# A down product in seven half-size products in place of eight, in a one-core hybrid decoder layer

## The chip, the cores and the metric

One core of one Trainium2 chip. The metric is the device time of one execution in microseconds (us). Engines: PE (matrix products, with its weight loads shown as PEld), DVE (vector), ACT (scalar), POOL (GpSimd), SP (which here only issues DMAs). A matmul here multiplies a stationary 128x128 block by a moving block of up to 512 columns and adds into a PSUM bank of 512 float32 columns.

## The reference, cut to what matters

One layer: three token mixers side by side, merged and added to the stream `z`, then a convolution FFN. 512 tokens, 1024 channels, 2816 hidden units; everything is float32 in and out. The change concerns the last line of the FFN:

```python
def _conv_ffn(h, w_up, conv_w, conv_b, w_down):
    u = h @ w_up                       # 1024 -> 2 x 2816
    ...                                # causal convolution over 3 tokens, per unit
    gate, val = c[..., :D_FF], c[..., D_FF:]
    return (jax.nn.silu(gate) * val) @ w_down     # 2816 -> 1024
...
z = z + _conv_ffn(_rmsnorm(z, ffn_norm[i]), ...)
return _rmsnorm(z, final_norm)[:, N_META:]
```

## The kernel before

Every float32 product is done as three float16 products: both operands are split into a high part (rounded by ACT) and a low part (the remainder, by DVE), and high x high, high x low and low x high are summed in PSUM.

The FFN has two parts. In the up part, 22 turns `f` (L1717) each compute two gemms of 128 hidden units (gate and value) over all tokens into a two-bank PSUM tile (`gbank()`, a ring of two such tiles, g0 and g1), ACT copies each result out into a tile `u` (`evac`, L414), DVE runs the convolution (L1712, L1714) into a tile `c`, ACT applies silu (L1732), DVE multiplies (L1733), and ACT and DVE split the result into the float16 tile `hid` (L1734, L1735): unit tile `f` in rows, 512 tokens in columns. The tiles of w_up come through `weights` (L227, L233, L234): load into one of three buffers `wf` (512 KB each, a ring), then split into one of three tiles `w`.

The down part loads the 22 tiles of w_down (128 units x 1024 channels, 512 KB each) through the same three `wf` buffers (L1746), splits each into its own place in `wd` (L1747 on ACT, L1748 on DVE), all 22 of which stay in SBUF. The product runs first for the token tiles 0 and 1: unit by unit, 12 matmuls for each, into four single banks `dn` (L1789). Then come token tiles 2 and 3, one half of the channels at a time, into g0 and g1 (L1797). A matmul's stationary operand is a 128-token block of `hid`, its moving operand a 512-channel half of `wd`. `finish_half` adds the product to `z` (L1765), squares it (L1767) and multiplies it by the final norm's weights `fnb` (L1770); `finish` adds the two halves' sums and takes the root on POOL (L1773, L1774), scales the halves on DVE and ACT (L1776, L1777) and stores them (L1780).

The engines run their queues in order. The order within each queue is set when the program is built: `TileContext(nc, schedule_with_timeline_sim=True)` takes instructions by their place in the text, and lets later ones go first where its own timeline sees the earlier one wait. The matmul calls go through the helper class `Paced`, so all matmuls have the line L101.

Of the kernel before, what the change touches and what calls it, by code (L numbers as in the profile page):

```python
# [9 lines left out]
F16 = mybir.dt.float16  # L10
# [8 lines left out]
P = 128  # L19
# [106 lines left out]
def trunk(ctx: ExitStack, tc: tile.TileContext, d: dict, out: bass.AP):  # L126
# [1565 lines left out]
    hid = fp.tile([P, 2, KF, SEQ], F16, name="hid")  # L1692
# [14 lines left out]

    def conv(j, ps):
        u = ft.tile([P, NY], F32, tag="u", name=f"u{j}")
        evac(u, ps, LATE, scale=IWS)  # L1710
        c = ft.tile([P, SEQ], F32, tag="c", name=f"c{j}", bufs=3)
# [5 lines left out]
    for f in range(KF):  # L1717
# [16 lines left out]
        act.activation(hid[:, 0, f], cv, AF.Copy)  # L1734
        vec.tensor_tensor(hid[:, 1, f], cv, hid[:, 0, f], op=ALU.subtract)  # L1735
# [4 lines left out]
    KF1 = 18  # L1740
    wd1 = fp.tile([P, KF1, 2, D], F16, name="wd1")
    wd2 = dq.tile([P, KF - KF1, 2, D], F16, name="wd2")
    wd = [wd1[:, f] for f in range(KF1)] + [wd2[:, f] for f in range(KF - KF1)]
    for f in range(KF):
        wf = take_wf().rearrange("p a b -> p (a b)")
        sp.dma_start(wf, d["w_down"][0][P * f : P * (f + 1), :])  # L1746
        act.activation(wd[f][:, 0], wf, AF.Copy, scale=WS)  # L1747
        vec.scalar_tensor_tensor(wd[f][:, 1], wf, WS, wd[f][:, 0], ALU.mult, ALU.subtract)  # L1748

    fnb = fp.tile([P, D], F32, name="fnb")  # L1750
    sp.dma_start(fnb, d["final_norm"].rearrange("(o c) -> o c", o=1).broadcast_to([P, D]))

    def down(pss, t, f, ss=(0, 1)):
        for j, (x, w) in enumerate(((0, 0), (0, 1), (1, 0))):
            for s in ss:
                pe.matmul(
                    pss[s], lhsT=hid[:, x, f, P * t : P * (t + 1)], rhs=wd[f][:, w, 512 * s : 512 * (s + 1)],
                    start=(f == 0 and j == 0), stop=(f == KF - 1 and j == 2),
                )

    def finish_half(pss, t, s, ss):
# [3 lines left out]
        vec.scalar_tensor_tensor(z, pss[s], IWS / HS, z, ALU.mult, ALU.add)  # L1765
        sq = ft.tile([P, NY], F32, tag="u", name=f"sq_{t}{s}")
        act.activation(sq[:, 0:512], z, AF.Square, scale=1.0 / 32, accum_out=ss[:, s : s + 1])  # L1767
        if s == 0:
            gps.tensor_scalar(ss[:, 0:1], ss[:, 0:1], EPS, None, ALU.add)  # L1769
# [12 lines left out]
    def sums(t):  # L1782
        return ft.tile([P, 2], F32, tag="ssf", name=f"ssf_{t}")


    pair = []
    for t in range(2):
        pair.append([bank(f"dn{t}{s}", P, 512) for s in range(2)])
    for f in range(KF):  # L1789
        for t in range(2):  # L1790
            down(pair[t], t, f)
    for t in range(2):
        ss = sums(t)
        for s in range(2):
            finish_half(pair[t], t, s, ss)
# [40 lines left out]
```

## Time and profile before

| | |
|---|---|
| median of 3 runs | 1013.29 us (1011.54 to 1013.64) |
| profiled execution | 1013.14 us, of which the span 1011.4 |
| PE, share of the span | 97% |
| DVE, ACT, POOL | 63%, 46%, 14% |
| granted PE clock, mean | 0.993 |
| HBM read | 86.92 MB |

Busy shares are averages over stages that have different limits, so what a change in one stage is worth is read in that stage: which engine works without a hole there, what the others wait for, and when the data that it needs are in place. Durations of pipelined instructions overlap: 264 matmuls of 379 ns each lie in 57 us.

### The profile page before, as it was taken

What the parts mean: (1) busy time and instruction counts of PE and PEld (TensorE: products, weight loads), DVE (VectorE), ACT (ScalarE), POOL (GpSimd) and SP (SyncE); (2) the same over time, 40 slices, a digit from 0 to 9 for tenths busy, and PEclk for the clock granted to TensorE, in tenths of its full rate; (3) what the DMA queues carried; (4) which work ended last, traced back from release to release, by engine and by line L of the source; (5) the groups of instructions that cost most, each with busy time, mean ns of one, the idle gap of its engine ahead of it and who ended that gap; (6) DMA issues with size and microseconds to landing.
All of it is one profiled execution on the core that took longest, in us unless ns stands there. A gap on an engine that the chain in (4) does not pass through costs nothing.

```text
span 1011.4 us, 20895 instructions
## 1 busy us (share of the span) xinstructions
PE 981.4 (97%) x8694; PEld 777.5 (77%) x8694; DVE 636.0 (63%) x1234; ACT 466.7 (46%) x881; POOL 136.8 (14%) x307
## 2 busy tenths in 40 slices
PE   8999999999999998999999999999999999999996
PEld 7888878888788777888888874488888888854442
DVE  5677655646678986767644494567776776872211
ACT  6867576347654344354433353643444344452100
POOL 3122221202335410111000032100000000000100
PEclk9999999999999999999999999999999999999999
DMA  6422222332244324122133562033233333573100
GB/s 194 108 64 63 66 66 82 84 84 80 79 111 108 92 73 91 39 64 64 43 84 94 183 206 66 1 105 104 87 103 105 104 92 98 161 218 101 42 21 21
DMA packets 149289, 92.35 MB, mean 91 GB/s; under 512 B 17664, under 2 KB 142073, under 8 KB 149195
## 3 DMA queue, kind: packets, MB, share of 16 engines
q1 hardware_dynamic: 149195, 91.02, 31.5%
q8 instruction: 68, 1.11, 0.5%
q14 instruction: 26, 0.21, 0.1%
HBM read 86.92 MB, written 3.95 MB: 90 GB/s over the span
## 4 chain that ended last, share of the span: by engine, by line
PE 78%; DVE 12%; ACT 5%; DMA 3%; issue 2%; POOL 1%; SPq 0%; POOLq 0%; DVEq 0%; ACTq 0%
PE g L101 60%; PE dn L101 6%; DVE w L234 2%; PE pc L101 1%; DVE HV L1222 1%; DVE AN L1227 1%; PE pf L101 1%; DVE wol L1606 1%; ACT w L233 1%; PE pw L101 1%; DMA s<-X 1%; ACT L414 1%; PE hT L106 1%; PE pogl L101 1%; PE pohg L101 1%
## 5 line engine op out<-in xcount | busy, mean ns | idle before, releaser
L101 PEld LDWEIGHTS <-w 128*128 128x128 f16 x5856 | 567.5, 98 | 86.1 <-issue 5.8
L101 PE MATMUL g<-hT,w 128*128 128x256 f16 (+3 forms) x5280 | 610.1, 274 | 1.3 <-DVE acc L478 0.6
L234 DVE SCALAR_TENSOR_TENSOR w<-wf,w 128x1024 f16<-128x1024 f32 (+1 forms) x131 | 150.5, 1150 | 91.5 <-ACT w L233 91.2
L233 ACT ACTIVATE w<-wf 128x1024 f16<-128x1024 f32 (+1 forms) x131 | 130.6, 999 | 109.7 <-PE g L101 100.2
L101 PEld LDWEIGHTS <-hid 128*128 128x128 f16 x528 | 51.7, 98 | 63.0 <-issue 1.1
L101 PE MATMUL g<-y,w 128*128 128x258 f16 x576 | 71.1, 273 | 1.4 <-DVE gate L478 1.3
L1714 DVE SCALAR_TENSOR_TENSOR c<-u,parB,c 128x512 f32<-128x512 f32 x88 | 66.0, 750 | 2.4
L101 PE MATMUL g<-wd,hid 128*128 128x512 f16 x264 | 57.3, 379 | 0.8 <-DVE z L1765 0.8
L101 PE MATMUL dn<-wd,hid 128*128 128x512 f16 x264 | 57.1, 379 | 0.0
L1769 POOL TENSOR_SCALAR ssf<-ssf 128x1 f32<-128x1 f32 x4 | 2.2, 540 | 311.2 <-ACT sq L1767 311.1
L101 PE MATMUL g<-woh,mT 128*128 128x512 f16 x128 | 38.9, 379 | 0.6 <-DVE z L1668 0.6
L1732 ACT ACTIVATE c<-c 128x512 f32<-128x512 f32 x22 | 13.8, 628 | 53.8 <-DVE c L1714 53.8
L1767 ACT ACTIVATE sq<-z 128x512 f32<-128x512 f32 x8 | 5.0, 628 | 71.5 <-DVE z L1765 71.5
L1748 DVE SCALAR_TENSOR_TENSOR wd<-wf,wd 128x1024 f16<-128x1024 f32 x22 | 26.9, 1223 | 16.5 <-ACT wd L1747 16.4
L101 PEld LDWEIGHTS <-mT 128*128 128x128 f16 x192 | 18.5, 98 | 24.2 <-issue 2.9
L1747 ACT ACTIVATE wd<-wf 128x1024 f16<-128x1024 f32 x22 | 23.2, 1057 | 25.9 <-DMA wf<-in_w_down_dram 25.9
L1765 DVE SCALAR_TENSOR_TENSOR z<-g,z 128x512 f32<-128x512 f32 x4 | 2.8, 692 | 45.8 <-PE g L101 45.8
L1468 POOL TENSOR_TENSOR gv<-gv,mhalf 128x2 f32<-128x2 f32 (+1 forms) x16 | 12.4, 779 | 128.3 <-DVE gv L1467 128.3
L414 ACT ACTIVATE u<-g 128x258 f32<-128x258 f32 x88 | 29.1, 372 | 0.0
L1497 ACT ACTIVATE HV<-pc 64x128 f32<-64x128 f32 x32 | 8.6, 270 | 36.6 <-DVE HV L1496 31.8
L101 PE MATMUL g<-wol,mT 128*128 128x512 f16 x64 | 24.3, 379 | 0.0
L1712 DVE TENSOR_SCALAR c<-u,parB 128x512 f32<-128x512 f32 x44 | 23.8, 541 | 0.0
(485 smaller groups left out, 1180.1 us busy)
## 6 DMA issues: line engine op xcount, KB each, us to landing
wf<-in_w_in_dram SPq DMA_DIRECT2D x65, 512.0 KB
wf<-in_w_up_dram SPq DMA_DIRECT2D x44, 512.0 KB
wf<-in_w_down_dram SPq DMA_DIRECT2D x22, 512.0 KB
wf<-in_w_out_dram SPq DMA_DIRECT2D x8, 512.0 KB
xt<-in_x_dram SPq DMA_DIRECT2D x4, 512.0 KB
wf<-in_w_out_hg_dram SPq DMA_DIRECT2D x8, 256.0 KB
wf<-in_w_out_gla_dram SPq DMA_DIRECT2D x8, 256.0 KB
wf<-in_w_out_rw_dram SPq DMA_DIRECT2D x8, 256.0 KB
```

Of the source, the lines that this page charges most:

```text
L101: r = self.eng.matmul(out, lhsT=lhsT, rhs=rhs, **kw)
L106: r = self.eng.transpose(out, in_, ident)
L233: act.activation(wh[:, :kt, :m], wf[:, :kt, :m], AF.Copy, scale=WS)
L234: vec.scalar_tensor_tensor(wl[:, :kt, :m], wf[:, :kt, :m], WS, wh[:, :kt, :m], ALU.mult, ALU.subtract)
L414: act.activation(dst[:m, off + c0 : off + c0 + n], src, func, **kw)
L1222: eng.tensor_tensor(u, bc(mats[:, j, j + 1 : n], c1 - c0), Ti[:, j, c0:c1].unsqueeze(1).broadcast_to([cnt, r, c1 - c0]), op=ALU.mult)
L1468: gps.tensor_tensor(var, var, mhalf[:, 0 : 2 * n].rearrange("p (a b) -> p a b", b=2), op=ALU.pow)
L1712: vec.tensor_scalar(c, u[:, 0:SEQ], colB(52 + j), colB(8 + j), ALU.mult, ALU.add)
L1714: vec.scalar_tensor_tensor(c, u[:, t : t + SEQ], colB(52 + 44 * t + j), c, ALU.mult, ALU.add)
L1732: act.activation(cg, cg, AF.Silu)
L1747: act.activation(wd[f][:, 0], wf, AF.Copy, scale=WS)
L1748: vec.scalar_tensor_tensor(wd[f][:, 1], wf, WS, wd[f][:, 0], ALU.mult, ALU.subtract)
```

## The change

The product Y = H W (H: tokens x units, W: units x channels) is computed block by block. H's blocks are halves of the tokens by the even and odd unit tiles of a pair; W's are the even and odd tile by halves of the channels. For each of 11 pairs:

- from H: A11, A12, A22 as they are, S1 = A21 + A22, S2 = S1 - A11, S3 = A11 - A21, S4 = A12 - S2 (`operands`, float32 sums on POOL, then all seven are split into high and low). `hid` holds seven blocks of 256 tokens for each pair;
- from W: T1 = B12 - B11, T2 = B22 - T1, T3 = B22 - B12, T4 = T2 - B21, and B11, B21, B22 as they are. `first_weights` makes T1 and T4 on POOL and T2 on DVE in place in `wf` and splits the two tiles; `last_weights` loads the odd tile again and half of the even tile, makes T3 on POOL and splits;
- seven products, each summed over the pairs in two banks (256 tokens x 512 channels): A11 B11, S2 T2, S1 T1, A22 T4 in a first stage; S3 T3 and S4 B22 in a second one, A12 B21 in a third. Between the stages ACT and DVE take the first four sums out of PSUM and add them to the four quarters of `z` as the scheme asks.

Split weights no longer stay for the whole product: 13 places (`NS1` + `NS2`) of a whole tile take turns. The tile `c` has four buffers in place of three. The load of `fnb` stands behind the first stage's.

```diff
@@ -1689,7 +1689,10 @@
     fctx = ExitStack()
     fp = fctx.enter_context(tc.tile_pool(name="ffn", bufs=1))
     ft = fctx.enter_context(tc.tile_pool(name="ffnt", bufs=2))
-    hid = fp.tile([P, 2, KF, SEQ], F16, name="hid")
+    HSEQ, KP = SEQ // 2, KF // 2
+    A11, A12, A22, S1, S2, S3, S4 = range(7)
+    hid = fp.tile([P, 2, KP, 7, HSEQ], F16, name="hid")
     w_up = d["w_up"][0]
     def up_gemm(j, ps, wt, spans):
@@ -1705,10 +1708,25 @@
     def up_weights(j):
         return weights(((w_up[:, P * j : P * (j + 1)], 0),), KD)
+    CB = 4
+    def operands(p, e, o):
+        e1, e2, o1, o2 = e[:, :HSEQ], e[:, HSEQ:], o[:, :HSEQ], o[:, HSEQ:]
+        sm = ft.tile([P, 4, HSEQ], F32, tag="sm", name=f"sm{p}", bufs=1)
+        gps.tensor_tensor(sm[:, 0], e2, o2, op=ALU.add)
+        gps.tensor_tensor(sm[:, 1], sm[:, 0], e1, op=ALU.subtract)
+        gps.tensor_tensor(sm[:, 2], e1, e2, op=ALU.subtract)
+        gps.tensor_tensor(sm[:, 3], o1, sm[:, 1], op=ALU.subtract)
+        for a, n, src in ((A11, 1, e1), (A12, 2, o), (S1, 4, sm.rearrange("p a t -> p (a t)"))):
+            h, l = (hid[:, x, p, a : a + n].rearrange("p a t -> p (a t)") for x in range(2))
+            act.activation(h, src, AF.Copy)
+            vec.tensor_tensor(l, src, h, op=ALU.subtract)
     def conv(j, ps):
         u = ft.tile([P, NY], F32, tag="u", name=f"u{j}")
         evac(u, ps, LATE, scale=IWS)
-        c = ft.tile([P, SEQ], F32, tag="c", name=f"c{j}", bufs=3)
+        c = ft.tile([P, SEQ], F32, tag="c", name=f"c{j}", bufs=CB)
         vec.tensor_scalar(c, u[:, 0:SEQ], colB(52 + j), colB(8 + j), ALU.mult, ALU.add)
         for t in (1, 2):
             vec.scalar_tensor_tensor(c, u[:, t : t + SEQ], colB(52 + 44 * t + j), c, ALU.mult, ALU.add)
@@ -1731,42 +1749,79 @@
         cg, cv = (conv(j, ps) for j, ps in zip(js, pss))
         act.activation(cg, cg, AF.Silu)
         vec.scalar_tensor_tensor(cv, cg, HS, cv, ALU.mult, ALU.mult)
-        act.activation(hid[:, 0, f], cv, AF.Copy)
-        vec.tensor_tensor(hid[:, 1, f], cv, hid[:, 0, f], op=ALU.subtract)
+        if f % 2:
+            operands(f // 2, cve, cv)
+        cve = cv
     h2ctx.close()
     dctx = ExitStack()
     dq = dctx.enter_context(tc.tile_pool(name="wd2", bufs=1, side="right"))
-    KF1 = 18
-    wd1 = fp.tile([P, KF1, 2, D], F16, name="wd1")
-    wd2 = dq.tile([P, KF - KF1, 2, D], F16, name="wd2")
-    wd = [wd1[:, f] for f in range(KF1)] + [wd2[:, f] for f in range(KF - KF1)]
-    for f in range(KF):
-        wf = take_wf().rearrange("p a b -> p (a b)")
-        sp.dma_start(wf, d["w_down"][0][P * f : P * (f + 1), :])
-        act.activation(wd[f][:, 0], wf, AF.Copy, scale=WS)
-        vec.scalar_tensor_tensor(wd[f][:, 1], wf, WS, wd[f][:, 0], ALU.mult, ALU.subtract)
+    NS1, NS2 = 10, 3
+    wd1 = fp.tile([P, NS1, 2, D], F16, name="wd1")
+    wd2 = dq.tile([P, NS2, 2, D], F16, name="wd2")
+    slots = [wd1[:, j] for j in range(NS1)] + [wd2[:, j] for j in range(NS2)]
+    NS = NS1 + NS2
+    nxt = 2 * KP % NS
+    take_slot = ring(NS, lambda j: slots[j])
+    take_t3 = ring(4, lambda j: slots[(nxt + j // 2) % NS][:, :, 512 * (j % 2) : 512 * (j % 2 + 1)])
+    take_last = ring(NS - 2, lambda j: slots[(nxt + 2 + j) % NS])
+    w_down = d["w_down"][0]
+    def rows(f, c0=0, n=D):
+        wf = take_wf().rearrange("p a b -> p (a b)")[:, :n]
+        sp.dma_start(wf, w_down[P * f : P * (f + 1), c0 : c0 + n])
+        return wf
+    def split_d(wf, w):
+        act.activation(w[:, 0], wf, AF.Copy, scale=WS)
+        vec.scalar_tensor_tensor(w[:, 1], wf, WS, w[:, 0], ALU.mult, ALU.subtract)
+        return w
+    lo, hi = slice(0, 512), slice(512, 1024)
+    def first_weights(p):
+        we, wo = rows(2 * p), rows(2 * p + 1)
+        gps.tensor_tensor(we[:, hi], we[:, hi], we[:, lo], op=ALU.subtract)
+        vec.tensor_tensor(wo[:, hi], wo[:, hi], we[:, hi], op=ALU.subtract)
+        gps.tensor_tensor(wo[:, lo], wo[:, hi], wo[:, lo], op=ALU.subtract)
+        we, wo = split_d(we, take_slot()), split_d(wo, take_slot())
+        return we[:, :, lo], we[:, :, hi], wo[:, :, hi], wo[:, :, lo]
+    def last_weights(p):
+        wo, wt = rows(2 * p + 1), rows(2 * p, 512, 512)
+        gps.tensor_tensor(wt, wo[:, hi], wt, op=ALU.subtract)
+        wo, wt = split_d(wo, take_last()), split_d(wt, take_t3())
+        return wo[:, :, lo], wo[:, :, hi], wt
     fnb = fp.tile([P, D], F32, name="fnb")
-    sp.dma_start(fnb, d["final_norm"].rearrange("(o c) -> o c", o=1).broadcast_to([P, D]))
-    def down(pss, t, f, ss=(0, 1)):
-        for j, (x, w) in enumerate(((0, 0), (0, 1), (1, 0))):
-            for s in ss:
+    def product(ps, a, w, p, ts=(0, 1)):
+        for t in ts:
+            for j, (x, y) in enumerate(((0, 0), (0, 1), (1, 0))):
                 pe.matmul(
-                    pss[s], lhsT=hid[:, x, f, P * t : P * (t + 1)], rhs=wd[f][:, w, 512 * s : 512 * (s + 1)],
-                    start=(f == 0 and j == 0), stop=(f == KF - 1 and j == 2),
+                    ps[t], lhsT=hid[:, x, p, a, P * t : P * (t + 1)], rhs=w[:, y],
+                    start=(p == 0 and j == 0), stop=(p == KP - 1 and j == 2),
                 )
-    def finish_half(pss, t, s, ss):
+    SC = IWS / HS
+    def add_to(t, s, v):
+        z = zt[t + 1][:, 512 * s : 512 * (s + 1)]
+        vec.scalar_tensor_tensor(z, v, SC, z, ALU.mult, ALU.add)
+    def finish_half(t, s, ss):
         hc = slice(512 * s, 512 * (s + 1))
         z = zt[t + 1][:, hc]
-        vec.scalar_tensor_tensor(z, pss[s], IWS / HS, z, ALU.mult, ALU.add)
         sq = ft.tile([P, NY], F32, tag="u", name=f"sq_{t}{s}")
         act.activation(sq[:, 0:512], z, AF.Square, scale=1.0 / 32, accum_out=ss[:, s : s + 1])
-        if s == 0:
-            gps.tensor_scalar(ss[:, 0:1], ss[:, 0:1], EPS, None, ALU.add)
+        if s == 1:
+            gps.tensor_scalar(ss[:, 1:2], ss[:, 1:2], EPS, None, ALU.add)
         vec.tensor_tensor(z, z, fnb[:, hc], op=ALU.mult)
     def finish(t, ss):
@@ -1780,29 +1835,58 @@
             sp.dma_start(out[0, P * t : P * (t + 1), hc], z[:, hc])
     def sums(t):
-        return ft.tile([P, 2], F32, tag="ssf", name=f"ssf_{t}")
-    pair = []
+        return ft.tile([P, 2], F32, tag="ssf", name=f"ssf_{t}", bufs=4)
+    def pair(name):
+        return [bank(f"{name}{t}", P, 512) for t in range(2)]
+    def gpair():
+        g = gbank()
+        return [g[:, 0, :], g[:, 1, :]]
+    q1, q6, q5, q4 = pair("q1"), pair("q6"), gpair(), gpair()
+    for p in range(KP):
+        b11, t1, t2, t4 = first_weights(p)
+        for ps, a, w in ((q1, A11, b11), (q6, S2, t2), (q5, S1, t1), (q4, A22, t4)):
+            product(ps, a, w, p)
+    sp.dma_start(fnb, d["final_norm"].rearrange("(o c) -> o c", o=1).broadcast_to([P, D]))
+    us = []
     for t in range(2):
-        pair.append([bank(f"dn{t}{s}", P, 512) for s in range(2)])
-    for f in range(KF):
-        for t in range(2):
-            down(pair[t], t, f)
+        u = ft.tile([P, SEQ], F32, tag="c", name=f"q16_{t}", bufs=CB)
+        v = ft.tile([P, SEQ], F32, tag="c", name=f"q165_{t}", bufs=CB)
+        act.activation(u, q1[t], AF.Copy)
+        vec.tensor_tensor(u, q6[t], u, op=ALU.add)
+        vec.tensor_tensor(v, q5[t], u, op=ALU.add)
+        us.append((u, v))
     for t in range(2):
-        ss = sums(t)
+        u, v = us[t]
+        z = zt[3 + t][:, lo]
+        vec.scalar_tensor_tensor(z, q4[t], -SC, z, ALU.mult, ALU.add)
+        for j, s, x in ((2 + t, 1, v), (2 + t, 0, u), (t, 1, v), (t, 0, q1[t])):
+            add_to(j, s, x)
+    b21s = []
+    for p in range(KP):
+        b21, b22, t3 = last_weights(p)
+        b21s.append(b21)
+        product(q6, S3, t3, p)
+        product(q5, S4, b22, p)
+    sss = [sums(t) for t in range(4)]
+    for t in range(2):
         for s in range(2):
-            finish_half(pair[t], t, s, ss)
-        finish(t, ss)
-    for t in range(2, 4):
-        g = gbank()
-        pss = [g[:, 0, :], g[:, 1, :]]
-        ss = sums(t)
-        for s in range(2):
-            for f in range(KF):
-                down(pss, t, f, (s,))
-            finish_half(pss, t, s, ss)
-        finish(t, ss)
+            add_to(2 + t, s, q6[t])
+            finish_half(2 + t, s, sss[2 + t])
+        finish(2 + t, sss[2 + t])
+    for t in range(2):
+        add_to(t, 1, q5[t])
+        finish_half(t, 1, sss[t])
+    for t in range(2):
+        for p in range(KP):
+            product(q1, A12, b21s[p], p, (t,))
+        add_to(t, 0, q1[t])
+        finish_half(t, 0, sss[t])
+        finish(t, sss[t])
     dctx.close()
     fctx.close()
```

## Rows read from the trace of the kernel before

**Rows 1.** The page's engine totals: busy us, share of the span, instructions.

```profile
PE 981.4 (97%) x8694; PEld 777.5 (77%) x8694; DVE 636.0 (63%) x1234; ACT 466.7 (46%) x881; POOL 136.8 (14%) x307
```

**Rows 2.** The chain that ended last, from 888 us: start, us, what.

```profile
888.71 56.98 PE dn L101 x264
945.70 42.75 PE g L101 x198
...
989.21 14.42 PE g L101 x66
...
1003.65 0.70 DVE z L1765
```

**Rows 3.** Busy us by stretch: PE, PEld, DVE, ACT, POOL; clock, DMA, GB/s.

```profile
864.00:889.00 25.00, 25.00 (x227) 21.81 (x225) 18.85 (x24) 13.07 (x22) 0.00 (x0) 1.00 0.55 169
889.00:905.00 16.00, 16.00 (x76) 7.26 (x75) 14.35 (x18) 9.20 (x13) 0.00 (x0) 1.00 0.75 233
905.00:925.00 20.00, 20.00 (x94) 9.06 (x93) 11.03 (x9) 8.69 (x9) 0.00 (x0) 1.00 0.60 181
925.00:944.00 19.00, 19.00 (x89) 8.62 (x88) 0.00 (x0) 0.00 (x0) 0.00 (x0) 1.00 0.00 1
```

**Rows 4.** The tile wd: instructions (ns min/median/max, starts); waits (us, times).

```profile
L1747 ACT ACTIVATE wd<-wf x22: 1056/1057/1057, 867.8 to 922.5; 128x1024 f16<-128x1024 f32 x22
L1748 DVE SCALAR_TENSOR_TENSOR wd<-wf,wd x22: 1214/1225/1226, 868.9 to 923.6; 128x1024 f16<-128x1024 f32 x22
...
  DMA wf<-in_w_down_dram: 25.9, 20
```

**Rows 5.** The timeline, 864 to 923: start us, us, engine, line; idle before, releaser.

```profile
864.31 55.22 SPq L1746 DMA_DIRECT2D wf<-in_w_down_dram  x22
...
867.80 1.06 ACT L1747 ACTIVATE wd<-wf 128x1024 f16<-128x1024 f32 x1 [0.35 <-DMA wf<-in_w_down_dram]
...
887.27 1.23 DVE L1748 SCALAR_TENSOR_TENSOR wd<-wf,wd 128x1024 f16<-128x1024 f32 x1 [2.48 <-ACT wd L1747]
...
888.41 0.64 ACT L414 ACTIVATE u<-g 128x258 f32<-128x258 f32 x2
...
893.52 0.64 ACT L414 ACTIVATE u<-g 128x258 f32<-128x258 f32 x2
...
904.18 1.06 ACT L1747 ACTIVATE wd<-wf 128x1024 f16<-128x1024 f32 x1 [1.34 <-DMA wf<-in_w_down_dram]
...
922.55 1.06 ACT L1747 ACTIVATE wd<-wf 128x1024 f16<-128x1024 f32 x1 [2.07 <-DMA wf<-in_w_down_dram]
```

**Rows 6.** SP's own waits, 855 to 930: us in total, times, longest.

```profile
SPq L1746 <- DVE wd L1748: 35.9, 19, 2.4
```

**Rows 7.** POOL by line: total us, mean ns; or ns min/median/max.

```profile
L645 POOL TENSOR_TENSOR skgl<-skgl,dcgl 128x4 f32<-128x4 f32 x6 | 1.3, 210 | 0.0
...
L1353 POOL TENSOR_TENSOR ARBK<-ident,gd x12: 607/622/2737, 348.1 to 418.8; 64x256 f32<-64x256 f32 x12
...
L1595 POOL COPY m<-mT x8: 181/1028/4667, 582.4 to 611.3; 128x2 f16<-128x2 f16 x8
```

**Rows 8.** The timeline of the longest POOL copy, with DVE beside it.

```profile
606.34 0.68 DVE L1594 TENSOR_TENSOR mT<-acc,mT 128x514 f16<-128x514 f32 x1
...
606.48 4.67 POOL L1595 COPY m<-mT 128x2 f16<-128x2 f16 x1 [0.56 <-ACT mT L1593]
...
606.94 1.22 DVE L234 SCALAR_TENSOR_TENSOR w<-wf,w 128x1024 f16<-128x1024 f32 x1
...
609.28 1.22 DVE L234 SCALAR_TENSOR_TENSOR w<-wf,w 128x1024 f16<-128x1024 f32 x1
...
610.42 0.68 DVE L1594 TENSOR_TENSOR mT<-acc,mT 128x514 f16<-128x514 f32 x1
```

**Rows 9.** Groups of DVE by line and shape: total us, mean ns, idle before.

```profile
L1735 DVE TENSOR_TENSOR hid<-c,hid 128x512 f16<-128x512 f32 x22 | 15.0, 684 | 0.0
...
L1765 DVE SCALAR_TENSOR_TENSOR z<-g,z 128x512 f32<-128x512 f32 x4 | 2.8, 692 | 45.8 <-PE g L101 45.8
```

## The prediction

> **What bounds the kernel now.** I read the engine totals first: PE is busy 97% of the span, DVE 63%, ACT 46%, POOL 14% [rows 1]. A total doesn't say what a stage waits for, so next comes the chain that ended last, for the stage that the change touches. From 888.7 us it is matmuls of the down product and hardly anything else: 264 in 56.98 us, 198 in 42.75, a 0.76 us hole, 66 in 14.42, and from 1003.65 the finishing of the last half tile [rows 2]. So 528 matmuls at 0.216 us each (56.98 / 264) set the end, and a tail of 1011.4 - 1003.65 = 7.8 us follows. The third view is by stretches: while the product runs, PE is busy all the time at full granted clock, DVE 75%, 90% and 55% in the three stretches in which w_down arrives, DMA 0.55 to 0.75, and from 925 on both are at rest: the weights are all in place 20 us before the first half of the product ends [rows 3]. The product is bound by PE and has a supply with room to spare. The question is whether that room outlives the change.
>
> **What goes.** 22 x 4 x 2 x 3 = 528 matmuls become 7 x 11 x 2 x 3 = 462 of the same shape (128 rows in, 512 columns): 66 x 0.216 = 14.3 us less on the bounding engine. The 0.76 us hole goes too: it was a half bank waiting for its neighbour's addition [rows 2], and the new last product uses separate banks. With PE never waiting, its end moves from 1003.65 to 888.7 + 462 x 0.216 = 988.5, and the profiled execution of 1013.14 (span 1011.4 and 1.74 around it; the median of three runs is 1013.29) becomes 1013.14 - 15.1 = 998.0. The tail stays: addition, square, two small POOL steps, scaling, two stores, as before.
>
> **What comes in the up stage.** Per pair of unit tiles 1792 columns are split into high and low part in place of 1024: DVE 0.684 us per 512 columns [rows 9], so 1.03 us more per 21 us of PE, ACT about the same, POOL four half-width operations. DVE has room for it (75% in the first stretch of rows 3, where the loads are added already), and nothing of this is needed before the pair's turn. I cost it at nothing; without that cover it would be at most 11 x 1.03 = 11 us.
>
> **What comes in the weight supply.** This is where the gain can go. In the kernel before, a tile of w_down takes a wf buffer, lands, and is split by ACT (1.057 us) and DVE (1.225) [rows 4]. SP's next load waits for that split: 35.9 us of its waiting [rows 6]; ACT in turn waits 25.9 us for landings [rows 4]. So the ring of three buffers sets the pace. Undisturbed: eight tiles from 904.18 to 922.55, 2.30 us a tile [rows 5], hence 6.9 us for one buffer's round, of which 2.3 are the split and 4.6 lie between release and landing. A load with the DMA engines to itself took 867.80 - 864.31 = 3.5 [rows 5]. The demand of PE was 12 x 0.216 = 2.6 per tile: the ring was faster.
>
> First stage after (four products, two whole tiles a pair): PE wants a pair every 24 x 0.216 = 5.2 us, the same demand. But a buffer is held longer. The even tile: POOL subtraction, ACT, DVE; the odd one: DVE subtraction (0.684), POOL subtraction, ACT, DVE. A POOL operation with two inputs of 512 columns isn't in the trace; the nearest rows are 210 ns at 4 columns and 607 at 256 [rows 7], a straight line through them gives 1.01 us at 512. Bounds: 0.61 (no dearer than half the width) to 2.74, the longest of the 256-column ones. I take 1.01. Then the even tile holds 1.0 + 1.06 + 1.22 = 3.3, the odd 0.7 + 1.0 + 1.06 + 1.22 = 4.0, and the ring delivers a pair every (3.3 + 4.0 + 2 x 4.5) / 3 = 5.4 us; with 0.3 us of waiting on each side, 5.6. The Trainium skill, page GPSIMD Engine Reference, section Elementwise — side-by-side cycle accounting, gives about 2.6 cycles an element for this operation, 4497 ns at 2048 columns; an estimate from that is 1.2 us at 512, and the pair would come every 5.8. No row here has that width.
>
> Where does it start? Before, the sixth tile (third pair) was split at 887.27 + 1.23 = 888.5 [rows 5], held back by the last w_up tiles in the same buffers. With three rounds each 1 to 1.7 us longer I put the third pair at 893.5, and the eleventh at 893.5 + 8 x 5.6 = 938. PE wants it at 888.7 + 10 x 5.2 = 940.6. The first stage just keeps up.
>
> Second stage (two products, 12 matmuls and 1.5 tiles a pair, all loaded a second time): PE wants a pair every 2.6 us. The odd tile holds its buffer 2.3, the half tile 1.0 + 0.6 + 0.7 = 2.3, and 0.3 of waiting; the landings take 4.5 and, for half the bytes, some 3.2 (bounds 1.8, half of the lone landing's 3.5, and 4.6): (2.3 + 2.6 + 4.5 + 3.2) / 3 = 4.2 us a pair. So PE outruns the supply by 1.6 us a pair. First pair ready 942, eleventh 942 + 10 x 4.2 = 984; the fourteen additions between the stages (0.69 us each, [rows 9], 9.7 us of DVE that stand in the same queue as the splits) I let cost 2, as DVE is free for half of each 4.2 us (none to 9.7): 986. PE then still owes 12 matmuls of that pair and the 66 of the last product: 986 + 2.6 + 14.3 = 1003, just where it ended before. That would be 1013.
>
> Against it works that the builder of the program orders each engine's queue along a timeline of its own, and lets later matmuls go first where it sees an earlier one wait; the last product's operands lie ready early. It can give back anything from nothing to the 14.8 us that PE waits. I take 3, the low end, because its timeline has the landings earlier than they are: that is why ACT stands waiting for them [rows 4]. Forecast: 1010.
>
> **The start of the product.** Its third and fourth quarter use the banks of the last two up products. ACT emptied these only at 888.41 and 893.52 (+0.64) [rows 5], 5 us behind PE, since it stood behind landings in ACT's queue. PE comes to the fourth after 18 matmuls, at 888.7 + 3.9 = 892.6, and waits at least 1.6 us, perhaps 6 as ACT's queue now also waits for POOL. Where supply sets the end this lies beside it and costs nothing; where it doesn't, it adds 1.6 to 6.
>
> **Rivals.** *Supply keeps up* (POOL nearer 0.6, landings nearer 3.5, or the waiting filled). First stage (2.9 + 3.6 + 7.6) / 3 = 4.7 a pair, second about 3.5: third pair 892, eleventh 930, second stage 933 + 35 = 968, ahead of PE. Then PE alone counts, with the wait at the start: 998.0 + 1.6 to 6, so 1000 to 1004. For it: DMA reached 233 GB/s [rows 3] where the second stage needs 0.77 MB / 2.6 us = 300 to keep pace, but it has a start of some pairs; against it: the three buffers.
>
> *POOL and DVE get into each other's way* (slower). A POOL copy of two columns, 181 ns alone, took 4667 [rows 7]: it began at 606.48 behind a dense run of two-input DVE instructions and ended as that run did [rows 8]. If every POOL subtraction waits for one split of 1.22, the even tile holds 1.2 longer, the odd 2.4, a pair comes 3.6 / 3 = 1.2 us later: 8 x 1.2 = 9.6 in the first stage, 11 x 0.4 = 4.5 in the second, 14 in all: 1024. For it: DVE is at 90% in 889 to 905. Against: from 905 it is at 55%, and it waits for POOL in this very chain. It decides from a mean wait of about 0.45 us a subtraction (5 us in all past my table). The Trainium skill, page SBUF — State Buffer, section Who interferes with whom, has it as an exclusive lock that the first comer holds for one instruction; by that rule POOL would wait one instruction at most, 1.2 us, and the row above shows more than one.
>
> *The change doesn't save matmuls or shifts work to the front*: the counts are plain from the code; left out but for a rest of 0.05, in which the up stage itself falls behind (DVE and ACT queues waiting for POOL), 1020 and above.
>
> **Numbers.** Forecast (supply sets the end, part of the wait filled) 0.45, 1005 to 1016, most at 1010; supply keeps up 0.28, 998 to 1005; POOL and DVE collide 0.22, 1017 to 1032, most at 1024; the rest 0.05. Range: 999 to 1026. By 0.2% a measurement can tell (1011.3 and 1015.3 around the median): faster 0.24 of the forecast's 0.45 and all of the second, 0.52; same 0.15; slower 0.06 + 0.22 + 0.05 = 0.33.
>
> **What would show it.** Right: PE without holes in the first four products but for one of some us at the fourth quarter, then holes of 1 to 2 us between groups of 12 matmuls, put down to the splits of the half tiles; pairs every 5.6 and then 4.2 us; the last 66 matmuls without holes. Wrong: no holes in the second stage (supply was faster), matmuls of the last product among those of the second stage (filled), POOL subtractions well over 1.0 us (collision), or holes before 888.

## The result and the profile after

The change made the kernel slower. Median 1027.80 us (four executions, 1026.75 to 1030.28) against 1013.46 for the kernel before beside it (1011.54 to 1015.22): ratio 1.0138, 95% interval 1.0123 to 1.0154. The profiled execution took 1026.90, of which the span is 1025.2.

The page's engine totals of the kernel after, and its HBM line (busy us, share of the span, instructions):

```profile
PE 974.2 (95%) x8628; PEld 772.5 (75%) x8628; DVE 705.8 (69%) x1292; ACT 496.7 (48%) x916; POOL 231.9 (23%) x384
...
HBM read 95.57 MB, written 3.95 MB: 97 GB/s over the span
```

The 66 matmuls are gone (8694 before, [rows 1]), POOL has 95 us more to do, DVE 70, and 8.65 MB more are read. No engine total says where the time is lost. The chain of waits does (start, us, what), beside [rows 2], where it was PE alone from 888 on:

```profile
656.55 210.69 PE g L101 x1904
...
870.25 3.49 DMA wf<-in_w_down_dram
...
900.46 4.58 DMA wf<-in_w_down_dram
...
905.17 1.59 POOL wf L1788
...
919.23 1.40 DVE wd L1780
...
934.87 4.39 DMA wf<-in_w_down_dram
...
953.51 5.33 DMA wf<-in_w_down_dram
...
1007.51 10.37 PE q L101 x48
```

Up to 867 the chain is PE's, and the up stage lost nothing. From 870 to 1007 PE has 2 us of it: landings of w_down have 42, DVE 53, POOL 19 and ACT 12, mostly splits and subtractions of weights. The product is bound by its supply. The stretches, in the columns of [rows 3] (busy us of PE, PEld, DVE, ACT, POOL; granted clock; DMA share; GB/s):

```profile
889.00:905.00 16.00, 16.00 (x75) 7.21 (x74) 15.93 (x18) 6.08 (x11) 6.39 (x4) 1.00 0.43 134
905.00:925.00 20.00, 16.06 (x60) 6.39 (x59) 13.89 (x11) 7.43 (x8) 14.65 (x10) 0.83 0.51 162
...
960.00:975.00 15.00, 3.28 (x8) 1.13 (x8) 10.23 (x11) 5.40 (x7) 4.47 (x4) 0.50 0.51 158
```

In 889 to 905 DMA moves 134 GB/s where it moved 233 [rows 3], through the same three buffers: they come free later. From 905 to 925 PE is busy 16 us of 20, and in 960 to 975 it does next to nothing. PE's own timeline shows the holes (start, us, matmuls; in brackets the wait before and what ended it):

```profile
910.17 1.24 PE L101 MATMUL q<-wd,hid 128*128 128x512 f16 x5 [0.43 <-DVE wd L1780]
913.07 0.38 PE L101 MATMUL q<-wd,hid 128*128 128x512 f16 x1 [1.66 <-ACT wd L1779]
915.30 2.29 PE L101 MATMUL q<-wd,hid 128*128 128x512 f16 x5 [1.86 <-DVE wd L1780]
917.39 4.57 PE L101 MATMUL g<-wd,hid 128*128 128x512 f16 x12
...
951.80 2.75 PE L101 MATMUL g<-wd,hid 128*128 128x512 f16 x12
971.72 11.15 PE L101 MATMUL q<-wd,hid 128*128 128x512 f16 x42 [17.17 <-DVE z L1815]
```

The account: with PE never waiting the product would have ended at 988.5; it ended at 1017.9, 29.4 us later. The first stage ends at 954.5 in place of 945.6 (8.9: waits of 0.43 + 1.66 + 1.86 + 0.62 + 0.31, 17 matmuls at the lower clock, 2.29 + 4.57 us where such groups take 1.24 + 2.75, and about 1 us in smaller pieces); then the hole of 17.2; then 3.4 (42 matmuls in 11.15 us where 42 x 0.216 is 9.1, and small waits). The tail is 1025.2 - 1017.9 = 7.3.

### The profile page after: what moved, and what is told of

It is laid out like the page before. It is cut to its first block, busy times and chain, and to the rows that moved or that the text cites. A ratio compares the mean times of both kernels' runs of the same rounds, so it can differ in the third digit from the quotient of the medians.

```text
span 1025.2 us, 21046 instructions
## 1 busy us (share of the span) xinstructions
PE 974.2 (95%) x8628; PEld 772.5 (75%) x8628; DVE 705.8 (69%) x1292; ACT 496.7 (48%) x916; POOL 231.9 (23%) x384
## 4 chain that ended last, share of the span: by engine, by line
PE 66%; DVE 15%; ACT 7%; DMA 6%; issue 2%; POOL 2%; SPq 0%; POOLq 0%; DVEq 0%; ACTq 0%
PE g L101 53%; DMA wf<-in_w_down_dram 4%; DVE wd L1780 2%; DVE w L234 2%; PE pc L101 1%; PE q L101 1%; DVE HV L1222 1%; DVE AN L1227 1%; ACT wd L1779 1%; POOL wf L1790 1%; PE pf L101 1%; ACT w L233 1%; PE pohg L101 1%; PE pw L101 1%; PE hT L106 1%
## 5 line engine op out<-in xcount | busy, mean ns | idle before, releaser
L234 DVE SCALAR_TENSOR_TENSOR w<-wf,w 128x1024 f16<-128x1024 f32 (+1 forms) x131 | 154.2, 1178 | 79.3 <-ACT w L233 75.0
L101 PEld LDWEIGHTS <-hid 128*128 128x128 f16 x462 | 46.3, 100 | 82.7 <-issue 32.5
L101 PE MATMUL q<-wd,hid 128*128 128x512 f16 x264 | 64.8, 392 | 23.0 <-DVE z L1815 17.2
L1780 DVE SCALAR_TENSOR_TENSOR wd<-wf,wd 128x1024 f16<-128x1024 f32 (+1 forms) x44 | 57.7, 1322 | 36.3 <-ACT wd L1779 36.3
L1779 ACT ACTIVATE wd<-wf 128x1024 f16<-128x1024 f32 (+1 forms) x44 | 41.5, 948 | 72.6 <-POOL wf L1790 26.2
L101 PE MATMUL g<-wd,hid 128*128 128x512 f16 x198 | 48.0, 390 | 0.0
L1719 POOL TENSOR_TENSOR sm<-c 128x256 f32<-128x256 f32 x11 | 8.8, 804 | 89.1 <-DVE c L1751 89.1
L1717 POOL TENSOR_TENSOR sm<-c,c 128x256 f32<-128x256 f32 x11 | 9.4, 855 | 86.3 <-DVE c L1751 86.3
L414 ACT ACTIVATE u<-g 128x258 f32<-128x258 f32 x88 | 28.3, 373 | 0.0
L1790 POOL TENSOR_TENSOR wf<-wf 128x512 f32<-128x512 f32 x11 | 20.7, 1880 | 20.9 <-DVE wf L1789 20.9
L1797 POOL TENSOR_TENSOR wf<-wf,wf 128x512 f32<-128x512 f32 x11 | 15.5, 1405 | 40.9 <-DMA wf<-in_w_down_dram 40.9
```

Source lines behind the costliest of these rows:

```text
L101: r = self.eng.matmul(out, lhsT=lhsT, rhs=rhs, **kw)
L234: vec.scalar_tensor_tensor(wl[:, :kt, :m], wf[:, :kt, :m], WS, wh[:, :kt, :m], ALU.mult, ALU.subtract)
L414: act.activation(dst[:m, off + c0 : off + c0 + n], src, func, **kw)
L1779: act.activation(w[:, 0], wf, AF.Copy, scale=WS)
L1780: vec.scalar_tensor_tensor(w[:, 1], wf, WS, w[:, 0], ALU.mult, ALU.subtract)
L1790: gps.tensor_tensor(wo[:, lo], wo[:, hi], wo[:, lo], op=ALU.subtract)
```

## The experiments

Two theories stood at first. *Supply*: the weights come too late whatever their order, so closing the hole only moves the wait. *Order*: the hole is an effect of the queues, in which the reads of the first four sums stand behind splits of later weights. Within supply there were two suspects: three buffers, and POOL and DVE getting into each other's way. Ratios are to the kernel before on the same chip, with the 95% interval; 0.001 is 1 us.

### The reads of the sums first

```diff
-        act.activation(u, q1[t], AF.Copy)
+        ia = act.activation(u, q1[t], AF.Copy).ins
-        vec.tensor_tensor(v, q5[t], u, op=ALU.add)
+        iv = vec.tensor_tensor(v, q5[t], u, op=ALU.add).ins
...
-        b21, b22, t3 = last_weights(p)
+        with ExitStack() as behind:
+            if p >= 1:
+                behind.enter_context(tc.issue_after(ia))
+                behind.enter_context(tc.issue_after(iv))
+            b21, b22, t3 = last_weights(p)
```

Expected: 

> Everything as in the changed kernel, but in the queues of DVE and ACT the splits of the second stage's weights from the second pair on stand behind the last read of the first stage's sums out of PSUM. Queue theory: the 17.2 us hole of PE between the stages is there because those reads stand behind splits whose weights have not landed; it falls below 3 us and the time by 10 to 14, to 1013 to 1018. Supply theory: the hole is only the place where the late weights show; it closes, but as much waiting comes back between the groups of the second stage, the last pair's T3 is still ready near 1000 to 1005, and the time stays at 1023 to 1028.

Measured: 1023.65, ratio 1.0089 (1.0066 to 1.0112), so 5 us less than the change alone. The hole of 17.2 is gone. PE's timeline of this kernel, two waits at the joint and two of the later ones:

```profile
958.52 1.89 PE L101 MATMUL q<-wd,hid 128*128 128x512 f16 x8 [0.28 <-DVE q L1860]
...
962.90 2.96 PE L101 MATMUL g<-wd,hid 128*128 128x512 f16 x13 [1.69 <-DVE q L1861]
...
979.24 1.24 PE L101 MATMUL g<-wd,hid 128*128 128x512 f16 x5 [1.37 <-DVE wd L1780]
...
1002.91 0.59 PE L101 MATMUL q<-wd,hid 128*128 128x512 f16 x2 [1.36 <-ACT wd L1779]
```

PE now waits for splits all through the second stage. Of 17.2 us, 5 were the queues' own; most of the rest had only collected in one place what the supply owed anyway. PE itself ends 5.9 us earlier (at 1012.0), but the tail behind it is 11.7 us in place of 7.3: only 13 matmuls of the last product are left at the end, and the chain leaves PE at 1008.4 for DVE's finishing of the sums.

### Without the second load

This kernel leaves out the second loads, the T3 subtractions and their splits; the second stage multiplies by what lies in the places.

```diff
-        wo, wt = rows(2 * p + 1), rows(2 * p, 512, 512)
-        gps.tensor_tensor(wt, wo[:, hi], wt, op=ALU.subtract)
-        wo, wt = split_d(wo, take_last()), split_d(wt, take_t3())
+        wo, wt = take_last(), take_t3()
```

Expected: 

> Leaves out the second stage's loads, its POOL subtractions and its splits: the products of the second and third stage read what the first stage left in the places. Both theories: no wait after the first stage but some 2 us for the reads out of PSUM; PE's end is the first stage's end (about 954) + 2 + 198 matmuls at 0.216 = 999, the time 1008 to 1010. The distance to the changed kernel, some 18 us, is the whole price of the second loading, hole included; the first stage's own lateness (7 to 8 us) stays. If the first stage ends earlier too, the two loadings disturb each other.

Measured: 1008.32, ratio 0.9940 (0.9923 to 0.9957). Its joint, from PE's timeline (the same view): the last product of the first stage, then the second without a wait.

```profile
951.43 2.75 PE L101 MATMUL g<-wd,hid 128*128 128x512 f16 x12
954.02 6.21 PE L101 MATMUL q<-wd,hid 128*128 128x512 f16 x28
```

The second load with all that hangs on it costs 20 us (1.0138 - 0.9940). The first stage ends at 954.2, as late as in the kernel after, so its 9 us have another cause.

### POOL's three subtractions on DVE

```diff
-        gps.tensor_tensor(we[:, hi], we[:, hi], we[:, lo], op=ALU.subtract)
+        vec.tensor_tensor(we[:, hi], we[:, hi], we[:, lo], op=ALU.subtract)
...
-        gps.tensor_tensor(wo[:, lo], wo[:, hi], wo[:, lo], op=ALU.subtract)
+        vec.tensor_tensor(wo[:, lo], wo[:, hi], wo[:, lo], op=ALU.subtract)
...
-        gps.tensor_tensor(wt, wo[:, hi], wt, op=ALU.subtract)
+        vec.tensor_tensor(wt, wo[:, hi], wt, op=ALU.subtract)
```

Expected: 

> The three weight subtractions of each pair move from POOL to DVE, nothing else. Port theory: POOL's 1.26 us subtractions stand 0.9 longer while a two-input DVE instruction runs (2.18 measured) and DVE's splits 0.75 longer behind POOL's; on DVE a subtraction takes 0.6 to 0.7, the pair's period in the first stage falls from 5.95 to 5.2 to 5.4, and the time to 1014 to 1021. Rival, the buffers' round (landing and three buffers) sets the period: it stays at 5.7 or more and the time at 1024 to 1028. Second rival, DVE becomes the bound: slower than 1028.

Measured: 1015.96, ratio 1.0023 (1.0013 to 1.0034): 11.5 us less. One view behind it is DVE's group of splits in 905 to 945 by form (count, busy us, mean ns, idle before). First the kernel after:

```profile
L1780 DVE SCALAR_TENSOR_TENSOR wd<-wf,wd 128x1024 f16<-128x1024 f32 x13 | 20.6, 1583 | 11.2 <-ACT wd L1779 11.2
```

Then with DVE subtracting:

```profile
L1780 DVE SCALAR_TENSOR_TENSOR wd<-wf,wd 128x1024 f16<-128x1024 f32 x15 | 18.3, 1219 | 1.9 <-ACT wd L1779 1.7
```

The same split takes 1.58 us beside POOL and 1.22 without it, so DVE does 15 splits and 21 subtractions where it did 13 and 6. PE's first stage ends at 947.9 in place of 954.5, and the hole shrinks from 17.17 us to 6.70:

```profile
954.65 12.72 PE L101 MATMUL q<-wd,hid 128*128 128x512 f16 x48 [6.70 <-DVE z L1815]
```

Some 6.4 us of that are given back, 3.7 in PE's later losses and 2.7 in the tail. One expectation missed: the pairs don't come every 5.2 to 5.4 us but every 5.81 (DVE's even subtractions from 913.17 to 936.40, four pairs), where they came every 5.95 beside POOL. DVE now waits for landings, 7.4 us in 905 to 945:

```profile
L1789 DVE TENSOR_TENSOR wf<-wf,wf 128x512 f32<-128x512 f32 x7 | 5.4, 765 | 3.4 <-DMA wf<-in_w_down_dram 3.3
...
L1788 DVE TENSOR_TENSOR wf<-wf 128x512 f32<-128x512 f32 x6 | 4.1, 690 | 4.1 <-DMA wf<-in_w_down_dram 4.1
```

Most of the lead was won before, where DVE had no time to spare (15.93 us busy of 16 in 889 to 905): the fifth pair's odd subtraction starts at 906.17 in place of 910.66, the eleventh's at 940.89 in place of 946.15. In the kernel after, the timeline of one pair shows how POOL and DVE meet:

```profile
924.80 1.27 POOL L1788 TENSOR_TENSOR wf<-wf 128x512 f32<-128x512 f32 x1 [0.75 <-DMA wf<-in_w_down_dram]
925.17 1.98 DVE L1780 SCALAR_TENSOR_TENSOR wd<-wf,wd 128x1024 f16<-128x1024 f32 x1 [2.24 <-ACT wd L1779]
927.14 0.69 DVE L1789 TENSOR_TENSOR wf<-wf,wf 128x512 f32<-128x512 f32 x1
927.75 1.22 DVE L1780 SCALAR_TENSOR_TENSOR wd<-wf,wd 128x1024 f16<-128x1024 f32 x1
927.91 2.18 POOL L1790 TENSOR_TENSOR wf<-wf 128x512 f32<-128x512 f32 x1 [1.84 <-DVE wf L1789]
```

POOL's even subtraction runs first: DVE's split, begun 0.37 us later, takes 1.98, its own 1.22 and nearly all that POOL had left. When DVE's own subtraction (L1789) ends, POOL's odd one is released and DVE goes straight on to its next split. DVE is first, and POOL takes 2.18, its own 1.26 and 0.92 of the 1.06 that the split had left. POOL's two prices for the same shape stand in the rows of its lines (ns min/median/max):

```profile
L1788 POOL TENSOR_TENSOR wf<-wf x11: 1262/1273/2277, 867.9 to 942.7; 128x512 f32<-128x512 f32 x11
...
L1790 POOL TENSOR_TENSOR wf<-wf x11: 1263/2176/2181, 874.6 to 946.1; 128x512 f32<-128x512 f32 x11
```

### Six buffers

Three tiles of the ring `w`, which the down stage doesn't use, join the three of `wf`; POOL keeps its subtractions.

```diff
+    bufs6 = [take_wf().rearrange("p a b -> p (a b)") for _ in range(3)]
+    bufs6 += [take_w().rearrange("p x a b -> p (x a b)").bitcast(F32) for _ in range(3)]
+    take_six = ring(6, lambda j: bufs6[j])
...
-        wf = take_wf().rearrange("p a b -> p (a b)")[:, :n]
+        wf = take_six()[:, :n]
```

Expected: 

> The w_down loads take turns in six landing buffers in place of three (the three tiles of the up part's split weights serve as the others); nothing else. Supply theory (landings and the ring set the pace): the splits come on time, the hole between the stages falls below 5 us, no waits for landings in the second stage, 1003 to 1010. Port theory: the first stage stays at 5.4 us a pair or more, as POOL and DVE need 2.5 + 0.6 + 2.2 us of each other's way; 1008 to 1015. Queue theory alone: the hole stays near 17 and the time at 1022 or more.

Measured: 1026.70, ratio 1.0125 (1.0110 to 1.0140): no gain that can be told. The stretch 905 to 925 of this kernel, in the columns of the stretches above, and two waits of PE's timeline, one ahead of that stretch and one between the stages:

```profile
905.00:925.00 20.00, 13.00 (x47) 5.11 (x46) 20.00 (x14) 7.86 (x8) 17.48 (x10) 0.83 0.55 183
```

```profile
896.59 1.71 PE L101 MATMUL g<-wd,hid 128*128 128x512 f16 x6 [3.00 <-ACT u L414]
...
972.18 11.82 PE L101 MATMUL q<-wd,hid 128*128 128x512 f16 x45 [6.05 <-DVE z L1819]
```

DVE is busy all 20 us with 14 instructions. That is no measure of its work: by the shortest durations of the same shapes in this trace, some 9 of the 20 us are waiting for POOL (an estimate). The buffers no longer pace the first stage, the two engines do. And "no gain" is a sum of two effects, which none of the theories had: the hole shrinks by 11 us, to 6.05, but the first stage ends at 966.1 in place of 954.5.

### The same with DVE subtracting

First the reads of the sums first and DVE subtracting (both diffs above):

Expected: 

> Subtractions on DVE and the reads out of PSUM ahead of the second stage's splits (from the second pair on), three buffers. With the subtractions on DVE the hole between the stages was 6.7 us. Queue theory: it goes and the time falls by 5 to 6, to 1009 to 1011. Supply theory: the waits move into the second stage, whose pairs still come every 4.5 us or so where PE wants one every 2.6; the time falls by no more than 3, to 1013 to 1017.

Measured: 1015.19, ratio 1.0007 (0.9996 to 1.0018), 1.6 us below the kernel with DVE subtracting alone, with intervals that overlap. With three buffers the order is worth little. PE ends 2.8 us earlier (1001.7 for 1004.5), but in both profiled executions the chain ends in the finishing of the sums behind the last splits (at 997.0 and 998.7), not in PE.

Then six buffers and DVE subtracting:

Expected: 

> Subtractions on DVE and six landing buffers. With POOL's subtractions six buffers gave nothing (1026.7 beside 1027.8), DVE being busy all the time from 905 to 925. Port theory: with POOL out of the chain DVE has room, so now the buffers are the limit, and six of them close the hole and the waits of both stages: 1001 to 1006. If landings never were a limit: 1014 to 1018 as with three.

Measured: 1005.32, ratio 0.9918 (0.9903 to 0.9933). Six buffers, worth nothing beside POOL, are worth 10.5 us without it. The first stage ends at 947.5, where it ended at 966.1 beside POOL. One hole of more than half a us is left in PE's timeline:

```profile
951.54 12.87 PE L101 MATMUL q<-wd,hid 128*128 128x512 f16 x48 [4.08 <-DVE z L1819]
```

Then all three, the reads ahead of the weights from the third pair of the second stage on:

```diff
+            if p >= 2:
```

Expected: 

> All three: subtractions on DVE, six buffers, reads out of PSUM ahead of the second stage's splits (from the third pair on). If each of the three causes costs something: PE without waits from 889 to 990, 999 to 1004, below the kernel before. If six buffers bring the splits in time anyway, the order of the queue makes no difference to the run with six buffers alone (within 2 us).

Measured: 1001.61, ratio 0.9885 (0.9868 to 0.9901). The hole is gone and its 3.7 us stay gained: here the order was the cause, as the supply is ahead. PE still waits three times in the first stage, 1.30 + 0.44 + 0.45 us. The stretch 905 to 925:

```profile
905.00:925.00 20.00, 18.70 (x87) 8.42 (x86) 16.69 (x22) 8.91 (x11) 8.90 (x3) 1.00 0.59 181
```

22 instructions of DVE in 16.69 us, where 14 took 20.00 with POOL subtracting.

### POOL busy beside, nobody waiting for it

To price the collision by itself: DVE subtracts, and POOL makes two subtractions a pair of the first stage on finished splits, into a tile `scr` that nothing reads.

```diff
         we, wo = split_d(we, take_slot()), split_d(wo, take_slot())
+        for w in (we, wo):
+            gps.tensor_tensor(scr, w[:, 0, lo], w[:, 0, hi], op=ALU.subtract)
```

Expected: 

> Subtractions on DVE, and beside them POOL does two subtractions a pair of the first stage, of the same size, on finished splits into a tile that nobody reads: POOL reads SBUF as in the changed kernel but nobody waits for it. Port theory: DVE's splits lengthen again (up to 2 us for 1.22), the first stage's pairs come later than every 5.6 us, and the time goes from 1016 to 1019 to 1024. Chain theory (POOL costs only because it stands in the chain, slower than DVE): within 2 us of 1016.

Measured: 1031.06, ratio 1.0176 (1.0158 to 1.0194): 15 us more than without them (1.0023) and more than the 1019 to 1024 expected, for work that no other instruction needs. The groups in 905 to 945 by form:

```profile
L1780 DVE SCALAR_TENSOR_TENSOR wd<-wf,wd 128x1024 f16<-128x1024 f32 x12 | 19.9, 1659 | 1.5 <-ACT wd L1779 1.5
L1795 POOL TENSOR_TENSOR scr<-wd 128x512 f32<-128x512 f16 x10 | 17.0, 1696 | 14.0 <-ACT wd L1779 13.7
```

DVE's split is at 1.66 again. No instruction waits for these subtractions in the trace, and the order of the queues is no rival here: ACT's is the same as without them, DVE's but for one exchange in the first stage. So it is not that the chain waits for a slow engine: POOL slows DVE by being at work. PE's first stage ends at 964.5 in place of 947.9.

### All three with POOL subtracting

The kernel of 1001.61 with the three subtractions back on POOL.

Expected: 

> Six buffers and reads first, but the subtractions on POOL as in the changed kernel. Port theory: POOL and DVE still hold each other up in the first stage (PE waited 15 us there with six buffers); only the 6 us hole between the stages can go: 1018 to 1024. If the port mattered only through the three buffers' round: near the 1001.6 of the same kernel with the subtractions on DVE, below 1006.

Measured: 1018.13, ratio 1.0049 (1.0034 to 1.0064). Its stretch 905 to 925:

```profile
905.00:925.00 20.00, 12.94 (x46) 5.04 (x45) 20.00 (x15) 6.98 (x7) 16.55 (x10) 0.83 0.50 162
```

With buffers and order mended, POOL's 33 subtractions turn a kernel that is 1.2% faster into one that is 0.5% slower: 16.4 us. All of it lies in the first stage, which ends at 968.4 in place of 949.2; there is no hole behind it.

### Nothing of the product's operands on POOL

The kernel of 1001.61, and the four sums of the up stage (`operands`) on DVE too:

```diff
-        gps.tensor_tensor(sm[:, 0], e2, o2, op=ALU.add)
+        vec.tensor_tensor(sm[:, 0], e2, o2, op=ALU.add)
```

and so for the other three.

Expected: 

> Subtractions on DVE, six buffers and reads first, and now also the four sums a pair of the up stage on DVE: POOL does nothing for the product any more. In the run with POOL's sums left, the last pair's first sum stood 7.45 us on POOL behind DVE, and PE waited 2.2 us for splits that stood behind it on ACT. Port theory: the waits go and the time falls by 1 to 3, to 998.5 to 1000.5. Rival, DVE gets too full in the up part (16.0 of 16 us busy from 889 to 905 already): 1001 to 1006.

Measured: 998.94, ratio 0.9865 (0.9849 to 0.9881), the fastest of all and better than both kernels. Its stretches, and its last matmuls:

```profile
905.00:925.00 20.00, 20.00 (x95) 9.09 (x93) 20.00 (x28) 11.58 (x13) 0.00 (x0) 1.00 0.67 219
925.00:945.00 20.00, 20.00 (x95) 9.04 (x94) 14.25 (x18) 8.76 (x11) 0.00 (x0) 1.00 0.62 200
```

```profile
981.04 7.93 PE L101 MATMUL q<-wd,hid 128*128 128x512 f16 x36
```

PE works from 889 to 989.0 without a wait, at the full clock. In 905 to 925 DVE is again busy 20 us of 20, but with 28 instructions, and DMA moves 219 GB/s where it moved 162 in the kernel after and 181 in the kernel before [rows 3].

The eight kernels that differ in three things only, as ratios:

| | three buffers | and reads first | six buffers | and reads first |
|---|---|---|---|---|
| POOL subtracts | 1.0138 | 1.0089 | 1.0125 | 1.0049 |
| DVE subtracts | 1.0023 | 1.0007 | 0.9918 | 0.9885 |

(with three buffers the reads stand ahead of the second pair's weights, with six of the third's). Each column falls by 8 to 21 us from the upper row to the lower. Six buffers are worth 10.5 and 12.2 us where DVE subtracts, 1.3 and 4.0 beside POOL; the order of the reads is worth 1.6 and 3.3 where DVE subtracts, 4.9 and 7.6 beside POOL. The builder orders the queues anew for each kernel, and in every column the traces have ACT's queue in another order above than below, so these prices include that; the kernel with POOL busy beside is the one that excludes it.

## Why the prediction was wrong, step by step

**The views and the bound: right.** PE bound the kernel before, and the saving is there: the sum gave 998.0 for a product in which PE never waits, and the last kernel above, in which it never does, has 998.45 in its profiled execution, with PE's end at 989.0 for 988.5. The up stage took nothing from PE, as costed, though its last sums on POOL fall into the product (906.73 to 910.7) and stand there ahead of a subtraction of the weights. With these off POOL too, the ratio goes from 0.9885 to 0.9865; the intervals overlap, but PE's last three waits are gone.

**The supply as the bound: right in kind, wrong in pace and cause.** I let the three buffers set the pace, a pair every 5.6 us, with the third pair ready at 893.5 and the eleventh at 938, just ahead of PE; behind the first stage I had PE wait 14.8 us, 3 of them filled. In the trace the third is ready at 900.4 (the split at 899.21 + 1.22), the later pairs come every 5.95 us (POOL's even subtractions from 918.85 to 942.67, four pairs), and the eleventh is ready at 950.7. PE lost 8.9 us in the first stage, where I had none, and 20.6 behind it, where I had 11.8. The failed step is "with 0.3 us of waiting on each side" around a POOL price of 1.01. Alone the subtraction takes 1.26, and beside DVE the odd one takes 2.18 from the sixth pair on, while DVE's split grows from 1.22 to 1.58 in the mean. But the collision isn't all of it. With DVE subtracting, at 0.69, and three buffers, the third pair is still ready only at 897.0, and the pairs come every 5.81: the round of the buffers, with its waiting, is itself longer than my 5.6. Two limits lie close together. With POOL subtracting, six buffers end the first stage later (966.1 for 954.5), so there the engines are the limit; without it they take the ratio from 1.0023 to 0.9918, so there the buffers were.

The Trainium skill, GPSIMD Engine Reference, section Elementwise — side-by-side cycle accounting, has the figure, about 2.6 cycles an element, behind the estimate of 1.2 us. That was nearer than my straight line through 4 and 256 columns: the trace has 1.26.

**The rival of the collision was the true case, and I gave it 0.22.** Its 14 us lie near what the runs show, 11.5 alone and 16.4 with buffers and order mended. That is partly luck: I had added 9.6 in the first stage and 4.5 in the second, and the two profiled executions, 10.7 us apart, differ by a first stage that ends 6.6 us sooner and a hole 10.5 smaller, less the 6.4 given back. Two sentences of mine spoke against it. "from 905 it is at 55%": the share of the kernel before says nothing of which instants are free. "it waits for POOL in this very chain": two tiles of a pair are in the chain at once. At the end of L1789 POOL's subtraction and DVE's next split start together, so they met in nearly every pair. I could have read this from the order of the statements in `first_weights` and `split_d`. And I counted only POOL waiting for DVE; it goes both ways, and by the groups of lines POOL's 33 subtractions (52.8 us) are 11 us longer than 33 x 1.26 and DVE's 33 whole splits (50.5) 10 us longer than 33 x 1.225.

The Trainium skill, SBUF — State Buffer, section Who interferes with whom, has a lock held for one instruction. In the pair shown above this fits: POOL waited 0.92, no longer than the 1.06 that DVE's split still had. The wait at the end of this document, 6.7 us in 7.45, is longer than one instruction. I had weighed it as a bound on POOL's wait; its sentence applies to either engine, and the cost here came from both.

**Why the range missed.** It ended at 1026, below the top of the rival's own 1017 to 1032, and the time is 1027.8. The rival's 1024 was 1010 and 14. The 14 came near; the 1010 didn't: without the collision the kernel takes 1016.0. There the step "the fourteen additions between the stages ... I let cost 2" fails, the second failed step. I priced them by their length on DVE (up to 9.7 us); what counts is where they stand in queues that run in order. The timeline of the kernel after shows the end of its 17.2 us hole:

```profile
968.03 1.06 ACT L1779 ACTIVATE wd<-wf 128x1024 f16<-128x1024 f32 x1 [0.45 <-DMA wf<-in_w_down_dram]
...
969.00 0.58 ACT L1859 ACTIVATE q<-q 128x512 f32<-128x512 f32 x1
969.12 1.95 DVE L1780 SCALAR_TENSOR_TENSOR wd<-wf,wd 128x1024 f16<-128x1024 f32 x1 [0.81 <-ACT wd L1779]
970.99 0.68 DVE L1815 SCALAR_TENSOR_TENSOR z<-q,z 128x512 f32<-128x512 f32 x1
971.59 0.68 DVE L1860 TENSOR_TENSOR q<-q,q 128x512 f32<-128x512 f32 x1
```

The sums are complete at 954.5. ACT's read of them (L1859) starts at 969.00, since ACT's queue holds, ahead of it, splits of weights that still have to land. The banks of the next products stay taken, so PE can do nothing, whatever lies ready. This is also why the planner's fill, for which I counted 3, couldn't shorten the hole: the third product needs a bank too. Of its 66 matmuls 18 did run ahead (48 come last), but behind the hole. With three buffers and DVE subtracting, the same hole is 6.7 us where I had 2, and 48 matmuls behind it take 12.72 us in place of 10.4; that is 4.7 and 2.3 us, where 1016 stands 6 above 1010. The tail is longer too, 10.0 us for 7.8. Smaller terms of both signs are left, which I did not take apart.

**The start of the product**: the wait for the fourth quarter's bank, 1.6 to 6 us, didn't come in the kernel after, as the second pair's first product had been put ahead of it. With six buffers it did come, 3.00 us (the row behind "ACT u L414").

**What would show it**: POOL subtractions well over 1.0 us were named as the sign of the collision, and holes between groups of 12 in the second stage as that of the forecast. The first came; the second only where no one hole hid it, in the kernel with the reads first. PE waited in the first four products, where the forecast had it wait for nothing but a bank, and 18 matmuls of the last product stood ahead, the sign named for filling.

## What to carry to other kernels

Work moved to an idle POOL is not free while DVE is on the path: look which DVE instructions run at the same instant, and let the one that comes second be longer by what the first has left (0.76 of 0.90 us and 0.92 of 1.06 in the pair shown). Here two POOL subtractions a pair that nobody waited for cost 15 us. An engine that is busy 100% with fewer instructions than before may be waiting, so read mean durations beside busy shares. A read that frees a PSUM bank is costed by what stands ahead of it in its engine's queue and what that waits for, not by its own length.

## What the hardware showed that I had not expected

POOL's wait isn't always one DVE instruction. In the kernel of 1001.61 a POOL addition of 256 columns, 0.72 us in the next row of the same timeline, took 7.45 while DVE ran two-input instructions one behind the other:

```profile
909.05 7.45 POOL L1717 TENSOR_TENSOR sm<-c,c 128x256 f32<-128x256 f32 x1 [13.18 <-DVE c L1751]
916.58 0.72 POOL L1718 TENSOR_TENSOR sm<-sm,c 128x256 f32<-128x256 f32 x1
```

[rows 8] have the same with 4.67. In the kernel after, POOL gets its turn behind a single instruction (2.18). That DVE runs there without a pause and here waits for ACT between two splits isn't enough to explain it: with six buffers beside POOL, DVE is busy 20.00 us of 20, and POOL's subtractions still took no more than 2.24 us in 905 to 920:

```profile
914.57 2.24 POOL L1792 TENSOR_TENSOR wf<-wf 128x512 f32<-128x512 f32 x1
```

It stays open. Nor is it only DVE's instructions with two inputs that lengthen: a TENSOR_SCALAR, which reads one tile and two columns of scalars, takes 0.54 us elsewhere and took 1.50 beside a POOL subtraction (897.01 in the kernel after).

PE's clock fell in two places where it had stood still. In 960 to 975, behind a hole of 17.2 us, the granted clock is 0.50, the lower of its two levels (1.2 GHz), and the first 42 matmuls take 2.1 us more than at the full one. Behind the waits of 0.43, 1.66 and 1.86 us at 909 to 915 the mean of the stretch is 0.83, and 12 matmuls take 4.57 us for 2.75. Behind the single wait of 1.69 us in the kernel with the reads first, 13 took 2.96, the full pace.
